# Sparse-expert layer in two blocks: token parts, one-hots, gathering and combining matrices about ten loop steps later

## The chip, the cores and the metric

The kernel runs on one core of a Trainium2 chip. The metric is the device time of one execution, in microseconds (us). The core's engines work side by side, each through its own instructions in a fixed order: PE (matrix products; its weight loads are listed as PEld), DVE (vector), ACT (scalar), POOL, and SP, which here issues nearly all transfers from the chip's memory (HBM) into on-chip buffers. An instruction waits for what it needs, and everything behind it on the same engine waits too.

## The reference

Two blocks of two layers each run over 256 tokens of width 1024. The first is attention alone. Each layer of the second is a mixer (sparse attention in layer 0, latent attention, MLA, in layer 1), a cross attention over 256 rows of memory, and a sparse mixture of 16 experts, which is what this case is about:

```python
def hier_moe(x, w_grp, b_grp, w_exp, b_exp, w_gate, w_up, w_down):
    '''Top-1 expert group, then top-2 experts within it; gate = p(group) * renormalised p(expert|group).'''
    def per_seq(xs):
        ...
        hdn = jax.nn.silu(jnp.einsum('sd,edf->sef', xs, w_gate)) * jnp.einsum('sd,edf->sef', xs, w_up)
        hdn = hdn * gate[..., None].astype(hdn.dtype)
        return jnp.einsum('sef,efd->sd', hdn, w_down)

def second_block(...):
    for i in range(DEPTH):                  # 2
        ...
        mkv = mem @ mem_w_kv[i]
        ...
        x = layer_norm(DEEPNORM_ALPHA * x + y, ln_g[i, 0], ln_b[i, 0])
        f = hier_moe(x, moe_w_grp[i], moe_b_grp[i], moe_w_exp[i], moe_b_exp[i],
                     moe_w_gate[i], moe_w_up[i], moe_w_down[i])
        x = layer_norm(DEEPNORM_ALPHA * x + f, ln_g[i, 1], ln_b[i, 1])
```

All is float32. A token uses 2 of 16 experts (width 1024, hidden 512).

## The kernel before

The function `moe` (L2362) emits one expert layer and is called twice: layer 0 at L2777 and layer 1 at L2782. Experts run in four groups of four (n = 4), each expert on up to 64 gathered rows.

**The loop.** `for s in range(16*NE+2)` (L2570) writes the program step by step, 16 steps for one expert; `at(pre, s, fn)` puts a piece of work ahead of step s's matrix products, `at(post, ...)` behind them. Gate and up products are `eg` (L2234), down products `dn` (L2274). PE, DVE, ACT and POOL take their orders from this loop in both layers; SP does so in layer 0, and in layer 1 a scheduler sets SP's order.

**What a group needs.** `x_parts` (L2524) splits the normalised tokens `xn` into a high part `xsh` (ACT, L2529) and the rest `xsl` (DVE, L2530), once in a layer, in four quarters. For each group after the first, `hots` (L2387, DVE) writes one-hot matrices `Dg` from token slots; the gather (PE, L2086) multiplies them with `xsh` and `xsl` into the group's rows `xg`, copied out of PSUM by ACT (L2091); `back` makes the combining matrices `dT` (transposes on PE L2112, casts on ACT L2119) and gates (L2121, DVE). `piece(s, it, m)` hands out the gather and `back` in slices; `open_expert` schedules all of it at steps relative to s = 16e, for the experts e = 2, 6 and 10.

**Weights.** Each expert's gate, up and down matrices, 2 MB each, come in loads of 512 KB: 192 loads in a layer (SP L119 and L2194). They land in three pools: a ring of 12 buffers of 512 KB (`w` in the profile), 8 buffers of 1 MB (`b8`) and 19 of 512 KB (`b4`); weights in the latter two are named `wa`. b8 and b4 serve other data as well (`xn`, `xsh`, `Dg`, `xg`, `dT`). `Weights.read` (L2205) frees a buffer at the last product that reads it, and issues the next load of a fixed list into it there and then; for b8 and b4 `may` (L2156) first counts, with the table `others` (L2144 to L2154) of (step, buffers taken or given back), whether the other users would run short, and if so leaves the buffer empty. So a load waits, through semaphores, for the PE instruction that frees its buffer, and SP issues loads strictly in program order. At most 8 loads are outstanding: each of SP's eight completion counters serves one at a time.

**The end of layer 0.** Expert 15's down matrix is loaded as four column quarters, 512 KB each (`moe_w_down 128x4x256`); `quarter(q)` (L2312, PE L2318) uses quarter q, and `add_quarter` (PE L2613) adds its result to the sum. At step 16*NE-19 = 237 of layer 0 the loop calls `tail`, which emits loads for the next layer: the memory's rows `memT` (L982, 1 MB), its four weight loads `wkv` (512 KB each) and four of MLA's input weights `w_in` (416 KB each). Behind quarter 3 PE goes on with the memory products `mkv` (L1000, L1004) and MLA.

Of the kernel before, what the change touches and what calls it, by code (L numbers as in the profile page):

```python
# [32 lines left out]
class Emit:  # L33


    def __init__(self, ctx, tc, aps, manual=False, nring=12, n8=8, n4=19, nw=3):
        self.tc, self.nc, self.a = tc, tc.nc, aps
        pool = lambda name, bufs, **kw: ctx.enter_context(tc.tile_pool(name=name, bufs=bufs, **kw))
        self.const = pool("const", 1)
        self.ring = pool("ring", nring)  # L40
        self.p8 = pool("p8", 1)
        self.p4 = pool("p4", 1)
        self.work = pool("work", 2)
        self.small = pool("small", 2)
        self.psum = pool("psum", 1, space=PSUM)
        self.slots = {"b8": list(range(n8)), "b4": list(range(n4)), "bank": list(range(8))}
        self.taken = {}
        self.lead = nw
        if manual:
            ctx.enter_context(tc.manual_schedule())  # L50
        nc = self.nc
        self.ident = self.const.tile([P, P], F32, name="ident")
        make_identity(nc, self.ident)
        self.sel = self.const.tile([P, 20], F32, name="sel")
        nc.vector.tensor_reduce(self.sel, self.ident.rearrange("p (j c) -> p c j", j=4)[:, :20], axis=AX.X, op=OP.add)
        self.mhalf = self.const.tile([P, 16], F32, name="mhalf")
        nc.vector.memset(self.mhalf, -0.5)
        self.one = self.const.tile([P, 1], F32, name="one")
        nc.vector.memset(self.one, 1.0)
# [2041 lines left out]
def back(E, Dg, gates, e0, new_dT, ga):  # L2101

    nc = E.nc
    n, m = Dg.shape[2], (gates.shape[1] - P) // 2
    for j0 in range(0, n, 2):
        js = range(j0, min(j0 + 2, n))
        ps = [E.bank()[:, :2 * (P + m)] for _ in js]
        for j, v in zip(js, ps):  # L2110
            for t in range(2):
                nc.tensor.matmul(v[:, (P + m) * t:(P + m) * t + P + m], Dg[:, t, j], gates[:, m * t:m * t + P + m],  # L2112
                                 start=True, stop=True)
        if j0 == 0:
            dT = new_dT()

        def out(js=js, ps=ps):
            for j, v in zip(js, ps):
                nc.scalar.copy(dT[:, j], v[:, m:m + 2 * P])  # L2119
                c = bass.AP(tensor=v.tensor, offset=v.offset + 2 * (e0 + j), ap=[list(v.ap[0]), [m + 2 * P, 2], [1, 2]])  # L2120
                nc.vector.tensor_reduce(ga[:, j:j + 1], c, axis=AX.XY, op=OP.add)  # L2121
            E.free(*ps)

        yield out


class Weights:
# [3 lines left out]
    def __init__(self, E, i):  # L2131
        self.E, self.i, self.m = E, i, [E.a[n][i] for n in ("moe_w_gate", "moe_w_up", "moe_w_down")]
        self.pieces = {(e, w): [] for e in range(NE) for w in range(3)}
        self.order = []
        for e in range(NE):
            at = ((e, 0), (e, 1), *[(e - 2, 2)] * 2, *[(e, 0), (e, 1)] * 2, *[(e - 1, 2)] * 2, (e, 0), (e, 1))
            self.order += [p for p in at if p[0] >= 0 and p != (NE - 2, 2)]
        self.order += [(NE - 2, 2)] * 4 + [(NE - 1, 2)] * 4
        self.unread, self.ring = {}, []


        self.early = [(1, 0), (1, 0)]
        self.step, self.last = 0, {"b8": {}, "b4": {}}
        self.others = {"b8": [(28, 2), (64, -1), (88, 1)], "b4": [(11, 1), (13, -1)]}  # L2144
        for s in (30, 94, 158):
            self.others["b4"] += [(s, 1), (s + 7, 1), (s + 19, 1), (s + 23, 1), (s + 30, -1), (s + 39, 1), (s + 55, 1)]
            self.others["b4"] += [(s + 62, -5)]
            self.others["b8"] += [(s + 69, 1), (s + 98, -1)]
        self.others["b4"] += [(226, 1), (229, 2), (232, 1), (235, 1), (238, -4), (245, 1), (257, 2)]
        if i == 0:  # L2150
            self.others["b8"].append((16 * NE - 19, 1))
            self.others["b4"].append((16 * NE - 19, 9))
        for v in self.others.values():
            v.sort(key=lambda e: (e[0], -e[1]))  # L2154
# [207 lines left out]
def moe(E, x, i, W, st, columns, sums, tail=None, overflow=True):  # L2362
# [17 lines left out]
    def new_hots(m):  # L2380

        return E.b4((2, m, 2 * CAP), "Dg", F32R)

    def hots(Dg, slots, h, j=0, ts=range(2)):
        m = slots.shape[2]
        for t in ts:
            nc.vector.tensor_tensor(Dg[:, t, j:j + m, h * CAP:h * CAP + CAP],  # L2387
                                    E.iota[:, None, :].to_broadcast([P, m, CAP]),
                                    slots[:, t, :, None].to_broadcast([P, m, CAP]), op=OP.is_equal)

    def new_group(m=n):

        return E.b8((KD, m, CAP), "xg"), []
# [16 lines left out]
    pre, post = {}, {}  # L2410

    def at(when, s, fn):
        when.setdefault(s, []).append(fn)
# [12 lines left out]
    groups, experts, ys = {}, {}, {}  # L2426
    made = {}

    def open_expert(e):
        s, j, g = 16 * e, e % n, e // n  # L2430
        xg, matrices = groups[g]
        X = experts[e] = (Expert if e < NE - 1 else LastExpert)(E, [W.pieces[e, w] for w in range(3)], W.read, xg, j,
                                lambda: matrices[1][:, j:j + 1])
        if j == 2 and e + 2 < NE:
            slots = slot[:, :, e + 2:e + 2 + n]

            def start():
                made["Dg"] = new_hots(n)
                hots(made["Dg"], slots, 0)

            def gen():
                yield from gather(E, made["xs"], made["Dg"], groups[g + 1][0])
                yield from back(E, made["Dg"], E.gates, n * (g + 1), *new_back(groups[g + 1]))

            it = gen()
            at(pre, s - 2, start)
            at(pre, s + 3, lambda: groups.__setitem__(g + 1, new_group()))

            for d, m in ((3, 4), (17, 2)):
                piece(s + d, it, m=m)  # L2450
            at(pre, s + 14, lambda: hots(made["Dg"], slots, 1))
            at(post, s + 28, lambda: E.free(made["Dg"]))
        if j == n - 1:
            at(pre, s + 16, lambda: E.free(xg))
        if e == NE - 1:
            return
        for d, fn in ((16, X.gate1), (17, X.gate2), (18, lambda: X.hidden1(0)), (19, lambda: X.hidden1(1)),
                      (20, X.hidden2)):
            at(pre, s + d, fn)
        if e == NE - 2:  # L2460
            return
        for d in range(2):
            at(post, s + 27 + 8 * d, lambda d=d: X.down(d))
        at(pre, s + 37, X.result1)
        at(pre, s + 38, X.result2)
        at(pre, s + 39, lambda: ys.setdefault(g, []).append(X.y))
        if j == n - 1:
            def gen(f):
                yield from combine(E, f, ys.pop(g), matrices[0], range(n), None if g else made["xs"])

            def start():
                if g == 0:
                    made["f"] = E.b8((2, D), "f")
                it = gen(made["f"])
                piece(s + 44, it, m=4)
                at(post, s + 44, lambda: E.free(matrices[0]))

            at(pre, s + 40, start)

    with tc.manual_schedule(engines=ENGINES if i else ENGINES | {mybir.EngineType.SP}):  # L2480
# [3 lines left out]
        xn = E.b8((2, D), "xn")  # L2484
        negate, shift, choose, slots, gates1, gates2 = router(E, lg, mv, r, *sums)
# [6 lines left out]
        Dg = new_hots(n)  # L2492
# [14 lines left out]
        for out in outs:  # L2507
            out()
        open_expert(0)
        for s in (1, 5):  # L2510
            piece(s, first)
# [13 lines left out]
        def x_parts(t, c):  # L2525
            if "xs" not in made:
                made["xs"] = E.b8((2, D), "xsh", F32R), E.b8((2, D), "xsl", F32R)
            hi, lo, src = (v[:, t, c] for v in (*made["xs"], xn))
            nc.scalar.copy(hi, src)  # L2529
            nc.vector.tensor_sub(lo, src, hi)  # L2530
# [9 lines left out]
                at(pre, 9 + 2 * m + t, lambda t=t, c=c, j=j: gain(t, c, j))  # L2540
        for k in range(4):
            t, c = k % 2, slice(512 * (k // 2), 512 * (k // 2) + 512)
            at(pre, 28 + 0 * k, lambda t=t, c=c: x_parts(t, c))
        at(pre, 35, lambda: E.free(xn))

        ps, work = {}, ()

# [22 lines left out]
        for s in range(16 * NE + 2):  # L2570
            W.step = s
            e, k = divmod(s, 16)
# [57 lines left out]
    if overflow:  # L2630
        with tc.If(most > CAP, label=f"overflow{i}"):
            with tc.For_i(0, NE, 1) as e:
# [12 lines left out]
                for b in range(1, S // CAP):  # L2645
                    nc.vector.tensor_scalar(sl, sl, -float(CAP), None, op0=OP.add)
                    Dg = new_hots(1)
                    hots(Dg, sl, 0)
                    hots(Dg, sl, 1)
                    g = new_group(1)  # L2650
# [4 lines left out]
                    for w, k, c in ((wg, D, FF), (wu, D, FF), (wd, FF, D)):  # L2655
                        p = E.wload(rows(w, k) if c == D else rows8(w), k, c)
                        m = 1024 // c
# [157 lines left out]
```

## Time and profile before

| | us |
|---|---|
| median of 3 runs (998.66 to 1002.4) | 1001.55 |
| the profiled execution's own time | 998.92 |
| its span in the trace | 997.2 |
| PE busy in the span | 971.9 (97%) |
| DVE busy | 641.6 (64%) |
| ACT busy | 435.7 (44%) |
| expert layer 0 in the trace, first to last expert product | about 444 to 659 |
| expert layer 1 | about 771 to 986 |

Times inside the trace count from the span's start; 1.72 us of the execution's time lie outside the span. The profile lists what each engine did, when, and what an instruction waited for; waits are inferred from semaphores. PE's ends are modelled, so a busy PE may be a PE that goes slowly.

### The profile page before, as it was taken

How to read it: one execution, taken by the hardware profiler on the slowest of the kernel's cores; microseconds unless marked ns; L12 is line 12 of the kernel's file. 1: busy time of each engine (PE TensorE's matmuls, PEld its weight loads, DVE VectorE, ACT ScalarE, POOL GpSimd, SP SyncE). 2: the span in 40 equal slices, each digit the busy share in tenths (PEclk: the TensorE clock that was granted, in tenths of full speed). 3: DMA queues.
4: the chain of work that ended last, by engine and by line, in shares of the span. 5: the costliest groups of instructions: out<-in, count | busy, mean ns of one | idle time of the engine just before them, and what ended most of it. 6: DMA issues, size and time to landing. Idle time of an engine off the chain costs nothing. (4 is left out here: it accounts for less than half of the span.)

```text
span 997.2 us, 16112 instructions
## 1 busy us (share of the span) xinstructions
PE 971.9 (97%) x5627; PEld 640.3 (64%) x5627; DVE 641.6 (64%) x1826; ACT 435.7 (44%) x1088; POOL 19.4 (2%) x40
## 2 busy tenths in 40 slices
PE   8999999999999989999999999999999999999995
PEld 8897889888897866775343443378867443434332
DVE  5857886557967788767456544467875645654455
ACT  6556664566664467653212121143875321212111
POOL 0000000000100000000000000000000000000000
PEclk9999999999999999999999999999999999999998
DMA  8963575443576584698999999977698899999995
GB/s 286 366 242 127 176 233 175 149 138 116 160 227 210 150 216 127 223 379 291 379 409 409 409 409 408 404 279 264 215 345 304 285 347 406 409 409 409 409 408 191
DMA packets 110889, 286.66 MB, mean 287 GB/s; under 512 B 14224, under 2 KB 30928, under 8 KB 110288
## 3 DMA queue, kind: packets, MB, share of 16 engines
q1 hardware_dynamic: 110800, 285.55, 79.8%
q8 instruction: 47, 0.77, 0.3%
q14 instruction: 42, 0.34, 0.1%
HBM read 284.46 MB, written 1.05 MB: 286 GB/s over the span
## 5 line engine op out<-in xcount | busy, mean ns | idle before, releaser
L2234 PE MATMUL eg<-wa,xg 128*64 128x512 f32 x792 | 204.9, 597 | 1.1 <-DMA wa<-moe_w_up_dram 0.8
L135 DVE TENSOR_TENSOR wsp<-w,wsp 128x512 fp32r<-128x512 f32 (+4 forms) x256 | 164.6, 656 | 64.0 <-ACT wsp L134 61.7
L253 PE MATMUL pj<-xTh,wsp 128*128 128x256 f32 x768 | 154.1, 291 | 1.7 <-ACT xTh L350 0.7
L134 ACT CAST wsp<-w 128x512 fp32r<-128x512 f32 (+4 forms) x256 | 142.3, 593 | 12.9 <-PE pj L253 5.7
L253 PEld LDWEIGHTS pj<-xTh,wsp 128*128 128x128 f32 x768 | 123.6, 191 | 9.0 <-issue 4.4
L2234 PEld LDWEIGHTS eg<-wa,xg 128*64 128x64 f32 x792 | 60.2, 137 | 107.1 <-issue 91.2
L2241 ACT ACTIVATE z<-eg 64x512 f32<-64x512 f32 x32 | 18.9, 592 | 210.2 <-PE eg L2234 210.2
L253 PE MATMUL pj<-xTl,wsp 128*128 128x256 f32 x384 | 108.6, 283 | 0.1
L253 PE MATMUL pj<-wsp,xTh 128*128 128x512 f32 (+3 forms) x352 | 108.5, 389 | 0.0
L2244 DVE SCALAR_TENSOR_TENSOR z<-z,eg 64x512 f32<-64x512 f32 x32 | 21.7, 679 | 127.6 <-ACT z L2241 127.6
L2254 DVE SCALAR_TENSOR_TENSOR hq<-z,gall,eg 32x128 f32<-32x128 f32 x240 | 83.4, 348 | 4.0
L2274 PE MATMUL dn<-wa,hT 128*64 128x512 f32 x348 | 83.8, 593 | 0.0
L253 PE MATMUL pj<-wsp,yTh 128*128 128x512 f32 x240 | 77.7, 405 | 0.0
L253 PEld LDWEIGHTS pj<-xTl,wsp 128*128 128x128 f32 x384 | 73.4, 191 | 0.7 <-DVE xTl L352 0.3
L2234 PE MATMUL eg<-w,xg 128*64 128x512 f32 x232 | 71.4, 595 | 0.2 <-DMA w<-moe_w_gate_dram 0.2
L253 PEld LDWEIGHTS pj<-wsp,xTh 128*128 128x128 f32 x352 | 62.8, 188 | 11.7 <-issue 2.5
L2285 ACT CAST ys<-dn 64x512 fp32r<-64x512 f32 x60 | 34.8, 580 | 75.5 <-PE dn L2274 65.5
L253 PE MATMUL pj<-wsp,xTl 128*128 128x512 f32 (+3 forms) x176 | 66.7, 379 | 0.0
L2274 PEld LDWEIGHTS dn<-wa,hT 128*64 128x64 f32 x348 | 24.7, 137 | 50.0 <-issue 42.7
L405 ACT ACTIVATE z<-z,mx 128x256 f32<-128x256 f32 (+1 forms) x104 | 48.1, 467 | 15.9 <-DVE mx L396 15.8
L2290 DVE TENSOR_TENSOR ys<-dn,ys 64x512 fp32r<-64x512 f32 x60 | 41.3, 689 | 12.3 <-ACT ys L2285 11.1
L253 PEld LDWEIGHTS pj<-wsp,yTh 128*128 128x128 f32 x240 | 43.1, 188 | 9.1 <-issue 1.6
(423 smaller groups left out, 1428.9 us busy)
## 6 DMA issues: line engine op xcount, KB each, us to landing
wa<-moe_w_up_dram SPq DMA_DIRECT2D x101, 512.0 KB, 10.2
wa<-moe_w_gate_dram SPq DMA_DIRECT2D x97, 512.0 KB, 10.2
wa<-moe_w_down_dram SPq DMA_DIRECT2D x93, 512.0 KB, 10.2
w<-w_in_dram SPq DMA_DIRECT2D x63, 512.0 KB, 5.0
w<-moe_w_down_dram SPq DMA_DIRECT2D x35, 512.0 KB, 10.2
w<-moe_w_gate_dram SPq DMA_DIRECT2D x31, 512.0 KB, 10.2
w<-moe_w_up_dram SPq DMA_DIRECT2D x27, 512.0 KB, 10.2
w<-w_out_dram SPq DMA_DIRECT2D x24, 512.0 KB, 3.6
```

Source lines behind the costliest of these rows:

```text
L134: self.nc.scalar.copy(hi, src)
L135: self.nc.vector.tensor_sub(lo, src, hi)
L253: nc.tensor.matmul(o, a, b, start=begin and i == 0, stop=last and i == 2, skip_group_check=True)
L405: E.nc.scalar.activation(z[i], (src or z)[i], AF.Exp, bias=mx[:, i:i + 1], scale=1.0 if src else -1.0, accum_out=sm[:, i:i + 1])
L2234: self.E.nc.tensor.matmul(self.ps[b * CAP:b * CAP + CAP], self.xg[:, k, self.j], w, start=k == 0, stop=k == KD - 1, skip_group_check=True)
L2241: self.E.nc.scalar.activation(self.th, self.ps[:CAP], AF.Tanh, scale=0.5)
L2244: self.E.nc.vector.scalar_tensor_tensor(self.th, self.th, 1.0, self.ps[:CAP], op0=OP.add, op1=OP.mult)
L2254: self.E.nc.vector.scalar_tensor_tensor(self.hq[32 * q:32 * q + 32, :, h], th[:, q], self.gate()[r], u[:, q], op0=OP.mult, op1=OP.mult)
L2274: self.E.nc.tensor.matmul(self.pd[n * CAP:n * CAP + CAP], self.hT[:, k], self.w[2][k](0)[:, 512 * n:512 * n + 512], start=k == 0, stop=k == 3,
L2285: self.E.nc.scalar.copy(self.y[r, n], self.pd[r])
L2290: self.E.nc.vector.tensor_sub(self.y[o, n], self.pd[r], self.y[r, n])
```

## The change

Three things are moved. The four `x_parts` come from step 28, all at once, to steps 39, 40, 41 and 42, one each, and `xn` is freed at 44 and not 35. For each following group (e = 2, 6, 10, s = 16e) the first half of the one-hots comes at s+10 and not s-2, the new group's buffers at s+13 and not s+3, the gather's four slices from s+13 and not s+3, the two slices of `back` from s+21 and not s+17, the second half of the one-hots at s+18 and not s+14; `Dg` is freed at s+22 and not s+28. The table `others` follows. No operation is added or removed.

```diff
-        self.others = {"b8": [(28, 2), (64, -1), (88, 1)], "b4": [(11, 1), (13, -1)]}
+        self.others = {"b8": [(39, 2), (64, -1), (88, 1)], "b4": [(11, 1), (13, -1)]}
         for s in (30, 94, 158):
-            self.others["b4"] += [(s, 1), (s + 7, 1), (s + 19, 1), (s + 23, 1), (s + 30, -1), (s + 39, 1), (s + 55, 1)]
+            self.others["b4"] += [(s + 7, 1), (s + 12, 1), (s + 23, 2), (s + 24, -1), (s + 39, 1), (s + 55, 1)]
             self.others["b4"] += [(s + 62, -5)]
-            self.others["b8"] += [(s + 69, 1), (s + 98, -1)]
+            self.others["b8"] += [(s + 79, 1), (s + 98, -1)]
...
-            at(pre, s - 2, start)
-            at(pre, s + 3, lambda: groups.__setitem__(g + 1, new_group()))
-
-            for d, m in ((3, 4), (17, 2)):
+            at(pre, s + 10, start)
+            at(pre, s + 13, lambda: groups.__setitem__(g + 1, new_group()))
+
+            for d, m in ((13, 4), (21, 2)):
                 piece(s + d, it, m=m)
-            at(pre, s + 14, lambda: hots(made["Dg"], slots, 1))
-            at(post, s + 28, lambda: E.free(made["Dg"]))
+            at(pre, s + 18, lambda: hots(made["Dg"], slots, 1))
+            at(post, s + 22, lambda: E.free(made["Dg"]))
...
-            at(pre, 28 + 0 * k, lambda t=t, c=c: x_parts(t, c))
-        at(pre, 35, lambda: E.free(xn))
+            at(pre, 39 + k, lambda t=t, c=c: x_parts(t, c))
+        at(pre, 44, lambda: E.free(xn))
```

How this moves instructions is seen at three places, all in layer 0. First PE at the gather for the second group (`xg<-Dg,xsh` and `xg<-Dg,xsl`, sixteen rows in all, of which two stand here; `eg` and `dn` are experts' gate, up and down products):

```order
 L2274 MATMUL dn<-wa,hT 64x512 x4
-L2086 MATMUL xg<-Dg,xsh 128x256 x2
-L2086 MATMUL xg<-Dg,xsl 128x256 x2
...
 L2234 MATMUL eg<-wa,xg 64x512 x8
 L2274 MATMUL dn<-wa,hT 64x512 x4
+L2234 MATMUL eg<-wa,xg 64x512 x2
+L2086 MATMUL xg<-Dg,xsh 128x256 x2
+L2086 MATMUL xg<-Dg,xsl 128x256 x2
```

The gather goes behind ten more gate and up products and four down products.

On DVE at the same place (`z`, `hq` and `hT` are an expert's hidden rows, `ys` its result, `xsl` the tokens' low part, `Dg` the one-hots):

```order
 L2262 STREAM_TRANSPOSE hT<-hq 128x256
+L2244 SCALAR_TENSOR_TENSOR z<-z,eg 64x512
+L2254 SCALAR_TENSOR_TENSOR hq<-z,gall,eg 32x4x32 x8
+L2262 STREAM_TRANSPOSE hT<-hq 128x256
+L2290 TENSOR_TENSOR ys<-dn,ys 64x512 x2
 L2530 TENSOR_TENSOR xsl<-xn,xsh 128x512 x4
 L2387 TENSOR_TENSOR Dg<-iota,slot 128x4x64 x2
 L2244 SCALAR_TENSOR_TENSOR z<-z,eg 64x512
-L2254 SCALAR_TENSOR_TENSOR hq<-z,gall,eg 32x4x32 x8
-L2262 STREAM_TRANSPOSE hT<-hq 128x256
-L2290 TENSOR_TENSOR ys<-dn,ys 64x512 x2
 L2387 TENSOR_TENSOR Dg<-iota,slot 128x4x64 x2
```

The four subtractions and the first one-hots go behind one more expert's hidden rows and its result.

On SP at the end of layer 0 (`128x4x256` are the four column quarters of expert 15's down matrix; `memT`, `wkv` and `w_in` belong to the next layer; `w` and `wa` name the pool of the buffer):

```order
 L119 DMA w<-moe_w_down_dram 128x1024 x4
-L119 DMA w<-moe_w_down_dram 128x4x256 x2
-L119 DMA wa<-moe_w_down_dram 128x4x256 x2
+L119 DMA w<-moe_w_down_dram 128x4x256 x3
 L982 DMA memT<-memT_dram 128x2048
 L119 DMA wkv<-mem_w_kv_dram 128x2x512 x4
 L119 DMA w_in<-mla_w_in_dram 128x2x416 x4
+L119 DMA wa<-moe_w_down_dram 128x4x256
 L2604 TENSOR_LOAD cnt_i
```

The third quarter takes a ring buffer, and the load of the last one goes behind all nine loads for the next layer.

## Rows read from the trace of the kernel before

**Rows 1.** Page, busy time of PE, and DMA's busy tenths in 40 slices.

```profile
PE 971.9 (97%) x5627; PEld 640.3 (64%) x5627; DVE 641.6 (64%) x1826; ACT 435.7 (44%) x1088; POOL 19.4 (2%) x40
...
DMA  8963575443576584698999999977698899999995
```

**Rows 2.** Windows: us; PE, PEld, DVE, ACT, POOL busy (instructions); PE clock; DMA share; GB/s.

```profile
470.00:480.00 10.00, 10.00 (x62) 5.96 (x62) 3.50 (x8) 3.51 (x6) 0.00 (x0) 1.00 1.00 361
480.00:490.00 10.00, 10.00 (x52) 3.86 (x50) 5.63 (x16) 2.95 (x7) 0.00 (x0) 1.00 1.00 374
490.00:600.00 110.00, 110.00 (x540) 45.51 (x538) 61.97 (x136) 22.87 (x43) 0.00 (x0) 1.00 1.03 409
...
800.00:820.00 20.00, 20.00 (x101) 7.74 (x101) 7.00 (x19) 4.56 (x10) 0.00 (x0) 1.00 0.98 340
```

**Rows 3.** Timeline of SP, end of layer 0: start, length, instruction, count.

```profile
643.05 4.39 SPq L119 DMA_DIRECT2D wa<-moe_w_down_dram  x2
647.55 2.03 SPq L982 DMA_DIRECT2D memT<-memT_dram  x1
649.62 2.36 SPq L119 DMA_DIRECT2D wkv<-mem_w_kv_dram  x4
652.39 6.07 SPq L119 DMA_DIRECT2D w_in<-mla_w_in_dram  x4
```

**Rows 4.** DMA issues between 657.7 and 657.9: KB, us from issue to landing.

```profile
w_in<-mla_w_in_dram SPq DMA_DIRECT2D x1, 416.0 KB, 10.7
```

**Rows 5.** Windows, as Rows 2, end of layer 0.

```profile
660.00:665.00 5.00, 5.00 (x27) 4.40 (x26) 2.74 (x8) 1.45 (x2) 0.70 (x1) 1.00 0.93 328
665.00:668.00 3.00, 3.00 (x20) 2.66 (x19) 2.05 (x4) 2.98 (x7) 0.00 (x0) 1.00 0.18 65
668.00:670.00 2.00, 2.00 (x13) 1.87 (x12) 1.97 (x5) 2.00 (x6) 0.00 (x0) 1.00 0.00 0
```

**Rows 6.** Timeline of PE, end of layer 0; an idle time before would stand in brackets.

```profile
656.79 1.08 PE L2318 MATMUL dn<-wa,hT 128*64 128x256 f32 x8
...
659.28 1.10 PE L1000 MATMUL mkv<-memT,wkv 128*128 128x256 f32 x4
```

**Rows 7.** Windows, as Rows 2, MLA's first part.

```profile
669.00:680.00 11.00, 11.00 (x56) 9.45 (x54) 10.55 (x22) 4.60 (x12) 0.00 (x0) 1.00 0.88 293
680.00:700.00 20.00, 20.00 (x140) 17.82 (x140) 14.31 (x50) 10.14 (x35) 1.62 (x3) 1.00 0.60 201
```

**Rows 8.** Windows, as Rows 2, where the granted clock fell.

```profile
764.00:766.00 2.00, 0.79 (x6) 0.74 (x7) 1.70 (x9) 2.00 (x3) 0.00 (x0) 1.00 1.01 389
766.00:767.00 1.00, 1.00 (x11) 0.95 (x10) 0.61 (x4) 1.00 (x1) 0.00 (x0) 0.65 0.90 369
767.00:768.00 1.00, 1.00 (x7) 1.00 (x7) 0.96 (x5) 0.18 (x1) 0.00 (x0) 0.50 0.27 111
768.00:769.00 1.00, 1.00 (x6) 1.00 (x6) 0.38 (x2) 0.00 (x0) 0.00 (x0) 0.50 0.60 176
769.00:770.00 1.00, 1.00 (x8) 1.00 (x7) 0.00 (x0) 0.00 (x0) 0.00 (x0) 0.64 0.95 254
```

**Rows 9.** Timeline of SP around the second group's gather in layer 0.

```profile
469.84 0.43 SPq L119 DMA_DIRECT2D wa<-moe_w_down_dram  x1
476.01 0.33 SPq L2194 DMA_DIRECT2D wa<-moe_w_gate_dram  x1
```

**Rows 10.** Timeline of PE, the same place: first gather row, and what follows the gather.

```profile
470.02 0.51 PE L2086 MATMUL xg<-Dg,xsh 128*128 128x256 f32 x2
...
474.05 3.22 PE L2234 MATMUL eg<-wa,xg 128*64 128x512 f32 x14
```

**Rows 11.** Timeline of DVE, the same place, before and during the gather.

```profile
462.74 2.46 DVE L2530 TENSOR_TENSOR xsl<-xn,xsh 128x512 fp32r<-128x512 f32 x4
465.12 0.75 DVE L2387 TENSOR_TENSOR Dg<-iota,slot 128x256 fp32r<-128x256 f32 x2
...
471.46 1.39 DVE L2290 TENSOR_TENSOR ys<-dn,ys 64x512 fp32r<-64x512 f32 x2
```

## The prediction

> **What bounds the kernel now.** I read the page first: PE is busy in 97% of the span, and the digits of DMA stand at 9 through long stretches and at 3 to 6 in others [rows 1]. So there are two resources that can set the end, and a stage has to be looked at by itself. In the windows, DMA is at its full rate, 409 GB/s, from 490 on, while at 470 to 490 (the second group's gather) it moves only 361 and 374, and in layer 1's like stretch 340 [rows 2]. PE is busy in all of these windows. The reader is to see that the expert layer starts with loads in hand and ends by living from hand to mouth: what the transfers lose early cannot be made up later.
>
> Then I read the end of layer 0, because there the order of SP changes most. Before, SP issues the last two column quarters of expert 15's down matrix from 643.05, and only behind them memT, the four wkv and the four w_in, the last of these between 657.7 and 657.9, at the end of the group that begins at 652.39 [rows 3, 4]. That last load takes 10.7 us from issue to landing [rows 4], so it lands at about 668.5; the windows agree, since DMA falls from 328 GB/s to 65 at 665 to 668 and to 0 at 668 to 670 [rows 5]. PE starts quarter 3 at 656.79 with no idle time ahead of it, and goes to the memory products at 659.28 [rows 6]. From there PE is busy without a gap to 700 [rows 5, 7] while DMA has slack [rows 5]: MLA's first part is bound by PE, so whatever holds PE up ahead of it moves everything behind it by as much.
>
> **The last quarter's load.** The change leaves the bytes as they are, but the load of quarter 3 now stands in SP's order behind memT, the wkv and the w_in. These are 1024 + 4 x 512 + 4 x 416 = 4736 KB, or 4.85 MB, and at the full rate of 409 GB/s [rows 2] that is 11.9 us. Worked out the other way: the same bytes are moved in the same stretch, so the one that now comes last lands when the last one landed before, at 668.5, and quarter 3 cannot start before that. Against 656.79 [rows 6] this is 11.7 us in which PE stands still, with quarter 3, the sums, the memory products and MLA in order behind it; ACT and DVE have the quarter's parts at the head of their own queues and wait with it. I take 11.7; the bytes give 11.9 as upper end. The lower end is 10.3: w_in and wkv now lie ready when PE goes on, and what ACT and DVE do to them may save MLA something, at most about the 1.4 us that quarter 3's own products and their sums leave ACT and DVE beside them (656.79 to 659.28 less the 1.08 us of the products [rows 6]). Nothing else covers the wait, because PE's order at this place is unchanged and PE has no other work to take.
>
> The Trainium skill speaks against this term: "DMA: Bandwidth & Descriptors", section "Queues, rings and completion order", says that completion is not in order for transfers issued by one engine, so that a later transfer's completion says nothing about an earlier one's. If that let the last quarter overtake, the wait would shrink towards nothing. In this trace transfers do drain in the order of issue as far as the end of the stretch shows it [rows 4, 5], and I let the trace decide.
>
> **The clock.** After an idle stretch PE may run at the lower clock. In 764 to 766 PE was busy 0.79 us of 2; then the granted clock was 0.65, 0.50, 0.50 and 0.64 in the four windows of 1 us that follow [rows 8]. That is 1.2 GHz instead of 2.4 in the middle two. At full clock the four would have held 0.35 + 0.50 + 0.50 + 0.36 = 1.7 us more of work. PE will stand idle much longer here, so I take 1.7 once, between 0 (no drop) and 3.4 (twice as long).
>
> **Gather and one-hots later.** The gather costs PE the same 4.03 us (470.02 to 474.05 [rows 10]), only 16e + 13 instead of 16e + 3. Before, SP had nothing free to issue from 469.84 to 476.01 [rows 9], since the loads behind wait for PE to pass the gather and the products that free their buffers. Those products now come ahead of the gather, so the loads go up to 4 us earlier; from 480 on, PE has done the same work either way, and a like gap of SP opens just behind. What it can give in layer 0 is bounded by what DMA lacks to its full rate here: 10 x (1 - 361/409) + 10 x (1 - 374/409) = 2.0 us [rows 2]. I take half, 1.0, because the new gap gives part of it back; bounds 0 and 2.0. In layer 1 the like stretch lacks 20 x (1 - 340/409) = 3.4 us [rows 2]; I take 1.0 of it, with 0 and 3.4 as bounds. The second and third gather of a layer lie where DMA is already full (409 GB/s at 490 to 600 [rows 2]), so I give them nothing. The gather itself issues no transfer, and no queue of SP or POOL is passed but by the loads just named.
>
> **x_parts later.** Four subtractions on DVE (2.46 us) and two one-hots (0.75) stood at 462.74 to 465.87, well ahead of the gather at 470.02 [rows 10, 11]. Now they stand behind expert 2's result, which ends at 471.46 + 1.39 = 472.85 [rows 11], so they end at 472.85 + 2.46 + 0.75 = 476.06. PE reaches the gather after ten products and four down products more. In the profile these are 20 and 8 records, and a record of a product takes 3.22/14 = 0.23 us [rows 10]; 28 of them after 470.02 end at 476.5, or at 476.0 if a record costs 0.215. So DVE is ready 0.4 us ahead or 0.1 us late. Cost: 0 to 0.1; I take 0. Behind the subtractions on DVE stand only the next expert's hidden rows, which wait for PE anyway. The copies of the gathered rows on ACT, the combining matrices and the second half of the one-hots move by 4 to 10 steps, and the first product that reads the new rows stands at step 65, so they cost nothing; that cover gone, a late `xg` would stop PE as a whole.
>
> **The sum.** 11.7 + 1.7 - 1.0 - 1.0 = 11.4 us. Against the profiled execution's 998.92 that is 1010.3. That execution lies 2.6 us below the median of 1001.55, and 1001.55 + 11.4 = 1013.0. I say 1012, nearer to the median.
>
> **Rivals.**
>
> The deeper queue alone (not slower). The last quarter is not held up: its packets go beside those of the nine loads ahead, or PE's wait is covered. Then only the leads are left: 998.92 - 2.0 = 996.9, or 999.6 from the median. With both leads at their bounds it is 998.92 - 2.0 - 3.4 = 993.5. For it speaks the skill's section above; against it that DMA ran dry just behind the last issue's landing, and that 8 loads at most are outstanding, so the quarter isn't even issued until w_in's loads are largely under way [rows 3, 4]. It decides from the point where the quarter lands before 656.79. Chance 0.11: 0.04 of it faster by more than 0.5%, 0.07 within 0.5%.
>
> The tail in part. The wait is there, but ACT and DVE use it to prepare MLA, and both leads come near their bounds: 11.7 - 1.4 + 0 - 2.0 - 2.0 = 6.3, so 1005.2 to 1007.9. For it speaks that w_in's loads now land ahead; against it that PE, not its inputs, sets MLA's pace [rows 5, 7]. Chance 0.15.
>
> DVE late at the gather. If the subtractions wait for a neighbour's rows as well, PE stands up to 2.46 + 0.75 = 3.2 us at the gather in each layer, the leads are gone, and the sum is 11.7 + 1.7 + 2 x 3.2 = 19.8: 1018.7 to 1021.4. Against it speaks the sum in x_parts above. Chance 0.06.
>
> **How the numbers follow.** The forecast has 0.68. About 0.5%, or 5 us, is what a measurement of this kernel tells from no change. The range runs from 1004 to 1017: its lower end takes the part-covered case (1005.2) and a clock that doesn't drop, its upper end 1002.4 + 11.9 + 3.4 = 1017.7 rounded down; left out are the deeper queue alone and DVE late, 0.17 in all. The forecast and the other two cases are slower by more than 0.5%, except for some 0.02 at the low edge: faster 0.04, within 0.09, slower 0.87.
>
> **What would show it.** In the changed kernel's trace SP's last load of layer 0's experts is one `wa` quarter behind the four w_in, with its landing about 10 us later; PE's row of quarter 3 has an idle time of 10 to 12 us ahead of it, released by that transfer, and the clock in the few us behind it is below 1. The window 470 to 480 moves more than 361 GB/s, and SP's gap from 469.84 is shorter. The prediction is wrong if quarter 3 starts before 660, if the memory products begin without idle time, or if the time from 669 to 700 in PE's work shrinks by several us because its inputs lie ready.

## The result, and the profile after

The changed kernel takes 1011.65 us (median of 6 runs, 1010.12 to 1012.69) against 1001.62 before (6 runs); the ratio is 1.0103, with a 95% interval of 1.0089 to 1.0118. The forecast was 1012.0. The profiled execution has a span of 1009.7 us, 12.5 more than before.

The page hardly shows why: PE has nearly the same busy time, in a longer span (before: [rows 1]).

```profile
PE 972.5 (96%) x5627; PEld 642.7 (64%) x5627; DVE 641.6 (64%) x1826; ACT 433.8 (43%) x1088; POOL 19.3 (2%) x40
```

SP's timeline at the end of layer 0 (start, length, instruction, count) answers to [rows 3]:

```profile
645.15 1.18 SPq L982 DMA_DIRECT2D memT<-memT_dram  x1
646.43 3.13 SPq L119 DMA_DIRECT2D wkv<-mem_w_kv_dram  x4
649.88 6.09 SPq L119 DMA_DIRECT2D w_in<-mla_w_in_dram  x4
656.73 0.58 SPq L119 DMA_DIRECT2D wa<-moe_w_down_dram  x1
```

The last quarter's load is issued at 656.73, and the row of DMA issues between 656 and 658 gives its time to landing, 10.8 us: it lands at 667.5.

```profile
wa<-moe_w_down_dram SPq DMA_DIRECT2D x1, 512.0 KB, 10.8
```

PE's timeline at the same place answers to [rows 6]:

```profile
655.04 0.74 PE L2613 MATMUL sum<-ys,dT 128*128 128x256 f32 x4
...
667.61 1.98 PE L2318 MATMUL dn<-wa,hT 128*64 128x256 f32 x8 [11.83 <-SPq L2631]
669.51 1.22 PE L2613 MATMUL sum<-ys,dT 128*128 128x256 f32 x4
670.89 1.19 PE L2613 MATMUL sum<-ys,dT 128*128 128x256 f32 x4
671.87 1.19 PE L1000 MATMUL mkv<-memT,wkv 128*128 128x256 f32 x4
...
673.33 1.03 PE L1000 MATMUL mkv<-memT,wkv 128*128 128x256 f32 x4
```

Before, the second row of memory products stands here:

```profile
660.65 1.03 PE L1000 MATMUL mkv<-memT,wkv 128*128 128x256 f32 x4
```

PE is through with the third quarter's work at 655.78, stands for 11.83 us, and starts quarter 3 when its load has landed. The bracket names SP's sequencer, not a DMA; the landing at 667.5 shows what it was. Quarter 3 now takes 1.98 us and not 1.08, and the memory products follow 4.26 us behind its start, before 2.49; their second row of L1000 follows 5.72 us behind it, before 3.86. The windows (us; PE, PEld, DVE, ACT, POOL busy; PE clock; DMA share; GB/s), which answer to [rows 5], show both halves: DMA works while PE stands, then PE works at the lower clock.

```profile
656.00:668.00 12.00, 0.39 (x2) 0.29 (x4) 0.71 (x3) 0.00 (x0) 0.00 (x0) 0.61 0.75 268
668.00:670.00 2.00, 2.00 (x10) 0.96 (x7) 0.00 (x0) 0.37 (x1) 0.00 (x0) 0.50 0.03 8
670.00:672.00 2.00, 1.85 (x9) 1.58 (x9) 0.74 (x2) 0.00 (x1) 0.00 (x0) 0.50 0.06 8
672.00:674.00 2.00, 2.00 (x11) 1.75 (x10) 1.68 (x7) 0.00 (x0) 0.21 (x1) 0.95 0.93 253
```

Before and after can be followed by three points on PE in each profile: from the first expert product of a layer to the transposes (L2306) ahead of the last expert's quarters, and from there to the memory products.

| us | layer 0, to L2306 | from there to the memory products | on to layer 1 | layer 1, to L2306 |
|---|---|---|---|---|
| before | 206.46 | 8.76 | 111.64 | 205.89 |
| after | 204.31 | 22.45 | 111.70 | 205.90 |

In these two profiles 13.7 us are lost at the last quarter, 2.1 are won in layer 0, and nothing in MLA or layer 1. The changed kernel's execution enters layer 0 1.05 us later (445.11 against 444.06), in code that is the same. Together that is 13.69 - 2.15 + 1.05 + 0.07 = 12.66 at the end of layer 1 (989.47 against 976.81).

### The profile page after: what moved, and what is told of

Its sections match the earlier page's. It is cut to its first block, busy times and chain, and to the rows that moved or that the text cites. A ratio compares the mean times of both kernels' runs of the same rounds, so it can differ in the third digit from the quotient of the medians.

```text
span 1009.7 us, 16115 instructions
## 1 busy us (share of the span) xinstructions
PE 972.5 (96%) x5627; PEld 642.7 (64%) x5627; DVE 641.6 (64%) x1826; ACT 433.8 (43%) x1088; POOL 19.3 (2%) x40
## 3 DMA queue, kind: packets, MB, share of 16 engines
HBM read 284.46 MB, written 1.05 MB: 283 GB/s over the span
## 5 line engine op out<-in xcount | busy, mean ns | idle before, releaser
L2234 PE MATMUL eg<-wa,xg 128*64 128x512 f32 x780 | 201.0, 596 | 0.5 <-DMA wa<-moe_w_up_dram 0.2
L2241 ACT ACTIVATE z<-eg 64x512 f32<-64x512 f32 x32 | 18.9, 590 | 196.5 <-PE eg L2234 196.5
L2274 PE MATMUL dn<-wa,hT 128*64 128x512 f32 x364 | 86.5, 593 | 2.0 <-DVE hT L2262 2.0
L2234 PE MATMUL eg<-w,xg 128*64 128x512 f32 x244 | 74.6, 595 | 0.2 <-DMA w<-moe_w_up_dram 0.2
L253 PE MATMUL pj<-wsp,yTl 128*128 128x512 f32 x120 | 47.1, 392 | 0.0
```

What stands on the lines that cost most here:

```text
L253: nc.tensor.matmul(o, a, b, start=begin and i == 0, stop=last and i == 2, skip_group_check=True)
L2234: self.E.nc.tensor.matmul(self.ps[b * CAP:b * CAP + CAP], self.xg[:, k, self.j], w, start=k == 0, stop=k == KD - 1, skip_group_check=True)
L2241: self.E.nc.scalar.activation(self.th, self.ps[:CAP], AF.Tanh, scale=0.5)
L2274: self.E.nc.tensor.matmul(self.pd[n * CAP:n * CAP + CAP], self.hT[:, k], self.w[2][k](0)[:, 512 * n:512 * n + 512], start=k == 0, stop=k == 3,
```

## The experiments

The theory at this point, A: the whole loss is the place of one load in SP's order, with the lower clock behind the idle time; the moved steps themselves win a little. The rivals: the moved steps cost something of their own (B, D), the late load waits for something other than the bytes ahead (C), the slow stretch behind quarter 3 is not the clock (F, G, H).

### e1: the changed kernel with the load ahead again

```diff
-            if tail and not work and s == 16 * NE - 19:
+            if tail and not work and s == 16 * NE - 17:
```

This puts the last quarter ahead of memT and changes no other order of loads: SP's loads stand in the trace as in the changed kernel's but for this one, and PE, DVE and ACT have the same order.

> The changed kernel with one edit: the next layer's nine loads at the end of layer 0 are emitted at step 239 and not 237, so that the last column quarter stands ahead of memT, wkv and w_in again. Theory A (the loss is the place of that load alone): the wait of 11.8 us at quarter 3 and the 1.8 us of lower clock behind it go, what stays is a lead of 1 to 2 us from the earlier loads: 999 to 1001 us against 1001.6 before. Theory B (the moved steps themselves cost something, DVE late at the gather or at an expert's hidden rows): 1003 us or more. In the trace A expects quarter 3 without idle time ahead of it, at about 655.8.

Measured: 998.59 us, ratio to before 0.9983 (0.9968 to 0.9997). On PE there is no idle time ahead of quarter 3:

```profile
656.83 1.08 PE L2318 MATMUL dn<-wa,hT 128*64 128x256 f32 x8
```

The loss is gone and a small gain is left, so A holds and B falls; the median lies 0.4 us under A's range. The start is at 656.83 and not 655.8 because layer 0 began 1.9 us later in this execution than in the changed kernel's.

### e2: the kernel before with the load behind

```diff
+                if (e, w, k) == (NE - 1, 2, 3) and self.hook:
+                    self.hook()
...
+        if tail:
+            W.hook = early
...
-            if tail and not work and s == 16 * NE - 19:
```

`early` emits the same nine loads, now from inside `Weights.load`, just ahead of the last quarter's. In the trace this moves one load of SP, and no instruction of PE, DVE or ACT changes its place.

> The kernel before with one edit: the next layer's nine loads are emitted between the third and the last column quarter, so that the last quarter comes behind them; no step of the loop is moved. Theory A: quarter 3 waits until about 668.5 in place of 656.8 and the clock falls behind it, 11.7 + 1.8 = 13.5 us more: 1015 us. Theory B (the loss needs the moved steps): within 2 us of 1001.6.

Measured: 1014.29 us, ratio 1.0128 (1.0106 to 1.0150). PE's timeline:

```profile
671.23 1.98 PE L2320 MATMUL dn<-wa,hT 128*64 128x256 f32 x8 [11.41 <-SPq L2637]
...
675.29 1.03 PE L1000 MATMUL mkv<-memT,wkv 128*128 128x256 f32 x4
```

The place of this one load alone makes the loss, with no step of the loop moved. It is 1014.29 - 1000.71 = 13.6 us.

### e3 and e8: fewer bytes ahead

e3 puts the quarter between the wkv and the w_in, e8 between memT and the wkv:

```diff
+            if tail and s == 16 * NE - 17:
+                tail[1]()
...
-                tail[1]()
```

(e8 emits the wkv at that step too, by a `yield` behind memT in `memory_kv`. In both, SP's order differs from the changed kernel's in this one load only.)

> The changed kernel with the last quarter behind memT and the four wkv, but ahead of the four w_in (4 x 416 KB = 1.70 MB, 4.2 us at 409 GB/s). Theory A (the wait is the bytes ahead, landed in order of issue): the wait shrinks from 11.8 to 7.7 us, and the time by 4.2 us to 1007.5. Theory C (the load waits for something else that is fixed, its buffer or a completion counter): the wait stays within 1 us of 11.8 and the time at 1011 to 1012.

> The changed kernel with the last quarter behind memT alone (1024 KB, 2.6 us at 409 GB/s), ahead of the four wkv and the four w_in. Theory A (the wait is the bytes ahead less what the load had in hand): with all nine loads ahead, 11.9 us of bytes, and with five, 7.7 us, PE waited 11.8 and 6.6 us; with one it waits about 1 us, at most 2.6, and so short an idle time costs little clock: 1000 to 1002 us, 1 to 3 more than with the quarter ahead of all (998.6). Theory C (something besides the bytes holds it): 1003 us or more.

Measured: e3 1007.25 us (ratio 1.0059, 1.0041 to 1.0076), e8 998.89 us (0.9985, 0.9970 to 1.0000). Quarter 3 in e3, and then in e8:

```profile
664.69 1.98 PE L2318 MATMUL dn<-wa,hT 128*64 128x256 f32 x8 [6.60 <-DMA wa<-moe_w_down_dram]
...
668.96 1.48 PE L1000 MATMUL mkv<-memT,wkv 128*128 128x256 f32 x3
```

```profile
658.01 1.08 PE L2320 MATMUL dn<-wa,hT 128*64 128x256 f32 x8 [0.92 <-DMA wa<-moe_w_down_dram]
```

| ahead of the quarter | MB | PE waits, us | median, us |
|---|---|---|---|
| nothing (e1) | 0 | 0 | 998.59 |
| memT (e8) | 1.05 | 0.92 | 998.89 |
| memT, wkv (e3) | 3.15 | 6.60 | 1007.25 |
| all nine (after) | 4.85 | 11.83 | 1011.65 |

The wait follows the bytes: A holds, C falls. The last 1.70 MB cost 5.2 us of wait and not 4.2, which is 326 GB/s and not 409. The changed kernel's windows show where the rest goes: 379 GB/s at 660 to 662, and then, with no load issued behind the quarter until 670.86, the transfers thin out before the quarter has landed at 667.5.

```profile
662.00:664.00 2.00, 0.00 (x0) 0.00 (x0) 0.00 (x0) 0.00 (x0) 0.00 (x0) 0.50 0.91 317
664.00:666.00 2.00, 0.00 (x0) 0.00 (x0) 0.00 (x0) 0.00 (x0) 0.00 (x0) 0.50 0.39 132
```

In e3, with four loads behind the quarter, the windows of 2 us from 660 until it lands move 364 and 373 GB/s. A's 1007.5 us for e3 came out by two misses that nearly cancel: the wait is 1.1 us shorter than 7.7, and the second row of L1000 follows quarter 3 by 6.45 us, 0.7 more than in the changed kernel. In e8 the wait is short and the clock stays up (quarter 3 takes 1.08 us); its cost is not to be told from e1, and its median lies 1.1 us under the expected 1000 to 1002.

### e4 and e5: each part of the change alone

e4 moves `x_parts` and the second group only, e5 the third and fourth group only; in e4

```diff
+            late = e in (2,)
+            at(pre, s + (10 if late else -2), start)
...
+            for d, m in (((13, 4), (21, 2)) if late else ((3, 4), (17, 2))):
```

and in e5 `(6,10,)` stands there; `others` follows. In both the column quarters are ahead of memT.

> The part alone: x_parts and the second group's one-hots, gather and combining matrices (e = 2) come later as in the change; the third and fourth group's (e = 6 and 10) stay where they were before. SP's order at the end of layer 0 is then that of before. Theory A: no wait at quarter 3, and the lead of the first gather in layer 0, about 1 us: 1000 to 1001 us. Theory B (moving x_parts behind an expert's result makes DVE late at the gather): 3 us more in each layer, 1005 to 1008 us.

> The other part alone: the third and fourth group's (e = 6 and 10) one-hots, gather and combining matrices come later as in the change; x_parts and the second group's stay where they were before. SP's four column quarters stand ahead of memT here. Theory A (only the first gather lies where the transfers have room, and the later ones give nothing): within 1 us of before, 1000 to 1002 us. Theory D (moving the gather of e = 6 away from the sums of the first group takes PE's cover from DVE, which shows as an idle time of 1.0 us ahead of a down product near 527 and near 852, and nothing makes up for it): 1 to 2 us more than before. Theory E (the lead of the changed kernel comes from these groups): 1 to 2 us less than before.

Measured: e4 999.02 us (ratio 0.9979, 0.9965 to 0.9992), e5 1001.02 us (0.9995, 0.9983 to 1.0008). The gain comes with e4's part, `x_parts` and the first gather together, as A has it (by the median 1.0 us more than A's range allows); the later groups give nothing. Which of e4's two moves gives it, no run separates. D's idle time is there, in e5 as in the changed kernel. PE's timeline in e5:

```profile
526.53 1.94 PE L2278 MATMUL dn<-wa,hT 128*64 128x512 f32 x8 [0.97 <-DVE hT L2266]
```

It comes again at 854.08, with 0.97 us, and e4 has neither. Before, PE did the third group's gather here, 4 us of work, while DVE added the first group's sums to the result (eight of 1.05 us each); now PE is at the down product before DVE has its rows. But it shows in no total: e5's interval ends at 1.0008, so D's 1 to 2 us more are excluded. E's 1 to 2 us less are not wholly (0.9983), but e4 has the gain without these groups.

### e6, e7, e9 and e10: what is slow behind quarter 3

e6 keeps PE busy through the wait:

```diff
+            if q == 3 and i == 0:
+                E.warm(84)
             X.quarter(q)
```

> The changed kernel, with 84 products of the identity with itself (128x128, into a PSUM bank that nothing reads) added on PE ahead of quarter 3 in layer 0, some 10 us of work inside the wait of 11.8 us. Quarter 3's load is as late as before. Theory A (1.8 us of the loss are the lower clock behind the idle time): quarter 3 starts at the same time, the memory products follow 2.5 us behind it and not 4.3, and the time falls by 1.8 us to about 1009.8. Theory F (the slow stretch behind quarter 3 comes from other things, the transfers that the next layer starts at that time or the engines' restart): 1011 to 1012 us.

Measured: 1017.13 us (ratio 1.0161, 1.0140 to 1.0182); a miss, because the products took twice what I had reckoned. PE's timeline:

```profile
659.38 18.92 PE L98 MATMUL warm<-ident 128*128 128x128 f32 x168
678.23 1.08 PE L2318 MATMUL dn<-wa,hT 128*64 128x256 f32 x8
...
680.71 1.05 PE L1000 MATMUL mkv<-memT,wkv 128*128 128x256 f32 x4
```

The time says nothing on the clock, but the stretch behind quarter 3 takes 2.48 us where the changed kernel takes 4.26. e7 has 46 products:

> As e6, but with 46 products: the 84 took 18.9 us and outlasted the wait, the memory products then followed quarter 3 by 2.5 us and not 4.3. At the 0.1126 us of one of its two records 46 take 10.4 us, inside the wait of 11.8 us. Theory A (1.8 us of the loss are the lower clock): quarter 3 starts when its load lands, the memory products follow 2.5 us behind, and the time is 1.8 us less than the changed kernel's 1011.65: about 1009.9. Theory F (the clock makes up for less, because what runs behind waits for other things as well): 1011 to 1012 us.

Measured: 1012.31 us (1.0107, 1.0088 to 1.0127); no gain over the changed kernel. PE's timeline:

```profile
668.61 1.08 PE L2318 MATMUL dn<-wa,hT 128*64 128x256 f32 x8 [0.60 <-SPq L2633]
...
672.20 0.99 PE L2613 MATMUL sum<-ys,dT 128*128 128x256 f32 x4 [1.84 <-PEq L2633]
672.98 1.91 PE L1000 MATMUL mkv<-memT,wkv 128*128 128x256 f32 x4
```

Quarter 3 runs at the full clock, then PE's own sequencer holds the last sum up by 1.84 us. Behind that second idle time the clock falls after all, and the memory products run at the lower level (a window, as above):

```profile
673.00:674.00 1.00, 1.00 (x4) 0.82 (x4) 1.00 (x4) 0.00 (x0) 0.00 (x0) 0.50 0.73 65
```

So in e7 the clock was held up to the branch only. Between the third quarter's sums and the last stands the branch that guards the second pass for experts with more than 64 rows. In e9 and e10 the branch and that pass are gone, in e9 from the changed kernel, in e10 from e7:

```diff
-def moe(E, x, i, W, st, columns, sums, tail=None, overflow=True):
+def moe(E, x, i, W, st, columns, sums, tail=None, overflow=False):
```

> The changed kernel without the second pass for experts that were chosen by more than 64 tokens, and without the branch on every engine that guards it (this part of the computation is left out). The branch stands on PE between the third and the fourth quarter's sums. With 46 filling products in the wait (e7) the clock was 1.00 at quarter 3, but PE then stood 1.84 us in front of the last sum, its own sequencer named as what it waited for, and nothing was won. Theory A (the wait for the load and the lower clock are what costs here, the branch only shows once the clock is held): quarter 3's wait stays near 11.8 us, the memory products follow 4.1 to 4.3 us behind its start, and the time is within 1.5 us of the changed kernel's 1011.65. Theory G (the branch is what makes the stretch behind quarter 3 slow): they follow 2.5 to 3 us behind, and the time is 1.5 to 2 us less.

> As e9, the branch and the second pass left out, with the 46 filling products of e7 in the wait. Theory A: the clock stays at 1.00, nothing else stands in the way, the memory products follow 2.5 us behind quarter 3's start, and the time is 1.8 us less than that of e9. Theory H (a PE that was kept busy is as slow behind the wait for other reasons): 4 us behind and the time of e9.

Measured: e9 1010.77 us (1.0084, 1.0060 to 1.0108), e10 1009.41 us (1.0074, 1.0048 to 1.0099). PE in e9, and then in e10:

```profile
668.76 1.97 PE L2318 MATMUL dn<-wa,hT 128*64 128x256 f32 x8 [11.06 <-DMA wa<-moe_w_down_dram]
670.66 2.08 PE L2613 MATMUL sum<-ys,dT 128*128 128x256 f32 x8
672.54 1.53 PE L1000 MATMUL mkv<-memT,wkv 128*128 128x256 f32 x4
...
674.34 1.03 PE L1000 MATMUL mkv<-memT,wkv 128*128 128x256 f32 x4
```

```profile
670.04 1.08 PE L2318 MATMUL dn<-wa,hT 128*64 128x256 f32 x8 [0.90 <-DMA wa<-moe_w_down_dram]
671.06 1.61 PE L2613 MATMUL sum<-ys,dT 128*128 128x256 f32 x8
672.51 1.03 PE L1000 MATMUL mkv<-memT,wkv 128*128 128x256 f32 x4
...
673.80 1.03 PE L1000 MATMUL mkv<-memT,wkv 128*128 128x256 f32 x4
```

Without the branch the stretch takes 3.78 us after an idle PE and 2.47 after a busy one, and the wait is put down to the DMA by name. But the clock has not come back yet at the first memory product of e9:

```profile
672.00:673.00 1.00, 1.00 (x6) 0.91 (x6) 0.65 (x2) 0.00 (x0) 0.00 (x0) 0.50 1.06 360
```

So the comparison has to go on to the second row of L1000: 5.58 us behind quarter 3's start in e9, 3.76 in e10. The clock by itself costs 1.8 us, as theory A had it. The medians differ by 1.36 us, but the intervals of these few runs overlap; the rows show the cause, the times are in keeping with it. With the branch in place, holding the clock up to quarter 3 wins nothing in e7: the branch then ends last, and the clock falls behind it. Theory G, the branch as the cause of the slow stretch, falls (3.78 us, and not 2.5 to 3), and so does H. Of the 0.5 us by which e9 is quicker than the changed kernel's 4.26, only 0.14 are left at the second row of L1000 (5.58 against 5.72). That is what these two executions leave for the branch; one of each doesn't settle it.

Without the branch SP, too, goes on: it issues MLA's next loads from 660.03 in e9, and only from 670.86 in the changed kernel. That is a second difference between the two, but it shows in no time of PE behind that row: from the second row of L1000 to layer 1 it is 110.25 us in e9, 110.14 in e10, 110.24 in the changed kernel and 110.27 before.

## Why the prediction was right, step by step

**The wait at the last quarter** was the right term with the right size: 11.7 was predicted, and PE stood for 11.83 us. Quarter 3's start moved by 10.82 (667.61 against 656.79), with the lead, which the sum took off apart, inside it. That the bytes in order of issue decide is shown by e2, e3 and e8. The Trainium skill, "DMA: Bandwidth & Descriptors", section "Queues, rings and completion order", says that completion does not follow the order of issue for one issuing engine; its example is a later transfer on one DMA engine beside an earlier one on sixteen, and the prediction stated it for transfers of every kind. It did not come to bear here: in e3, e8 and the changed kernel the quarter landed in the place in which it was issued. MLA gave nothing back (111.64 and 111.70 us to layer 1), nor in e9 and e10, where its loads come some 10 us earlier, so the lower end of 10.3 was not needed.

**The clock** was put at 1.7 us, and the stretch behind quarter 3 became 1.86 longer up to the second row of L1000 (5.72 less 3.86), where the clock is back. It was right in size and in cause: e9 and e10, with PE idle and PE kept busy in the wait, differ there by 1.82. The size is in part luck, as it was taken from one fall elsewhere in the trace, and it depends on when the clock comes back: by the same measure e2 lost 1.50 us to before, and e3 2.59. The prediction had not read the branch on PE beside it, which shows as 0.14 us between e9 and the changed kernel, one execution each, and as 1.84 us in e7.

**The leads** were put at 1.0 and 1.0. From one pair of profiles they would be 2.15 and 0. Over all twelve they are steadier: to L2306, layer 0 takes 206.75 us on average in the three without the first group's move (before, e2, e5: 206.46 to 207.25) and 204.84 in the nine with it (203.51 to 206.34); layer 1 takes 205.97 (205.89 to 206.05) and 205.18 (204.46 to 205.90). That is 1.9 and 0.8 us, so the term for layer 0 looks too small and that for layer 1 about right; the nine differ among themselves by 2.8 us in layer 0, so the 1.9 is rough. By the medians' ratios to before, e4 has 2.1 us in all and e1 1.7, against 2.0 in the sum.

The windows that the bound of layer 0 came from did fill up (before: 361 and 374, [rows 2]):

```profile
471.05:481.05 10.00, 10.00 (x62) 5.71 (x58) 5.92 (x12) 3.92 (x7) 0.00 (x0) 1.00 1.01 399
481.05:491.05 10.00, 10.00 (x52) 3.88 (x52) 6.32 (x18) 4.38 (x10) 0.00 (x0) 1.00 1.02 410
```

That is nearly the whole bound of 2.0, not half of it; the new gap of SP (nothing issued from 479.01, the end of the group that begins at 476.28, to 482.24) took little, since DMA stayed at 410 GB/s through it:

```profile
476.28 2.73 SPq L119 DMA_DIRECT2D wa<-moe_w_down_dram  x2
482.24 0.33 SPq L2194 DMA_DIRECT2D wa<-moe_w_gate_dram  x1
```

In layer 1 the new gap did give part of the gain back. The windows before, and then after (12.65 us later, as layer 1 is):

```profile
790.00:800.00 10.00, 10.00 (x60) 5.19 (x57) 7.85 (x18) 5.10 (x9) 0.00 (x0) 1.00 0.86 293
800.00:810.00 10.00, 10.00 (x55) 4.41 (x55) 2.63 (x6) 2.49 (x6) 0.00 (x0) 1.00 0.96 323
810.00:820.00 10.00, 10.00 (x48) 3.33 (x48) 4.37 (x14) 2.06 (x5) 0.00 (x0) 1.00 0.99 358
```

```profile
802.65:812.65 10.00, 10.00 (x50) 3.36 (x48) 5.54 (x13) 3.56 (x7) 0.00 (x0) 1.00 1.01 373
812.65:822.65 10.00, 10.00 (x62) 5.70 (x60) 4.21 (x9) 2.88 (x6) 0.00 (x0) 1.00 0.95 316
822.65:832.65 10.00, 10.00 (x52) 3.88 (x50) 5.02 (x16) 2.88 (x8) 0.00 (x0) 1.00 0.98 336
```

The first window moves 80 GB/s more, the next two 7 and 22 less: 10 x (80 - 7 - 22)/409 = 1.2 us of transfers are left of 2.0.

**x_parts and the gather.** The tie was real. On DVE the subtractions run at 473.94 and the one-hots end at 477.11:

```profile
473.94 2.50 DVE L2530 TENSOR_TENSOR xsl<-xn,xsh 128x512 fp32r<-128x512 f32 x4
476.36 0.75 DVE L2387 TENSOR_TENSOR Dg<-iota,slot 128x256 fp32r<-128x256 f32 x2
```

and PE starts the gather at 477.09, with no idle time named:

```profile
477.09 0.53 PE L2086 MATMUL xg<-Dg,xsh 128*128 128x256 f32 x2
```

So the rival "DVE late at the gather" did not come. What the prediction missed is DVE late elsewhere, at the down product near 526, where the gather's 4 us had covered it.

**The sum** had 11.4 us and the medians differ by 10.0, which the larger lead in layer 0 (0.9 us more than in the sum) would explain in part; that the forecast of 1012 lies so near is partly luck. The sum was set on a profiled execution 2.6 us below the median. Of the twelve profiles it is the only one in which PE kept the full clock just ahead of layer 0, as the last section shows; so part of its 2.6 us is not to be expected of another execution, and the prediction, which split the difference, went by judgement there.

## What to carry to other kernels

Where an engine issues transfers in a fixed order, look for what a moved step does to the order at the far end of the layer: a load that gets its buffer two steps later can fall behind a whole batch for the next layer, and its price is the bytes ahead of it at the rate of that stretch, and the clock that falls while PE waits. Emitting that batch two steps later cost nothing and turned 1.0% slower into 0.2% faster than before (e1); the first group's part alone does as well (e4). Filling an idle time with work to hold the clock wins nothing if something else, here a branch, ends as late and lets the clock fall behind it (e7). And whoever prices a lower clock has to measure up to the point where it is back.

## What the runs showed of the hardware that was not expected

Behind a wait for a transfer, PE's sequencer can need more than the clock does: in e7, 1.84 us in front of the first product behind a branch, with the granted clock at 1.00 until then and at 0.50 behind it; after 18.9 us of other work in e6 the same branch cost nothing that the trace shows. What the sequencer does in that time no run here shows.

Executions of code that does the same up to there start the expert products of layer 0 at 444.06 to 447.82 us. The last eight products of L2075 just ahead took 1.14 us in the profile of before and 1.77 to 2.06 in the eleven others. PE's timeline of e2 stands for these:

```profile
442.09 2.06 PE L2075 MATMUL xg<-Dg,xn 128*128 128x128 f32 x8
```

So a term of a microsecond or two can't be read from one pair of profiles at that place.
